# Feature projections of a two-layer decoder trunk: three 256-column matmuls into one accumulator, and tiles moved by 192 bytes

## The chip, the cores and the metric

The kernel runs on one core of a Trainium2 chip. The metric is the device time of one execution in microseconds (us). PE is the tensor engine's matmul stream, PEld its weight loads, DVE the vector engine, ACT the scalar engine, POOL GpSimd, SP the engine that issues most DMAs.

## The reference

Two layers, 256 tokens, 1024 features, all in float32. Cut to what matters:

```python
for l in range(2):
    proj = x @ w_in[l]                      # 1024 -> 6912 features: q, k, v of two attentions, three conv inputs, three gates
    y_a = sliding_window_attention(a_q, a_k, a_v, sinks, slopes)
    u = b_c * b_h                           # gated short convolution, 512 channels, 3 taps
    y_b = b_b * (u[-2] * cw[0] + u[-1] * cw[1] + u * cw[2])
    y_c = moba_attention(c_q, c_k, c_v, slopes)      # 256 tokens: one causal block
    mix = (sigmoid(g_a) * (y_a @ w_br_a) + sigmoid(g_b) * (y_b @ w_br_b) + sigmoid(g_c) * (y_c @ w_br_c)) @ w_out[l]
    x = layer_norm(sqrt(2) * x + mix)
    ffn = (silu(x @ w_gate) * (x @ w_up)) @ w_down   # 1024 -> 2816 -> 1024
    x = layer_norm(sqrt(2) * x + ffn)
```

## The kernel before

**Numbers in two parts.** Every operand of a projection is held as two tiles of the type float32r: a high part, written by ACT (`halve`, `parts`), and a low part, the difference, made by DVE. A product is the sum of three matmuls: high by high, low by high, high by low.

**Pieces.** The weights lie in memory as 140 pieces (70 a layer) of 128 x 2048 float32, 1 MB each, in the order of their use. SP loads a piece into one of three `raw` tiles; ACT and DVE split it in two chunks of 1024 columns into one of four pairs `wh`, `wl` (line 182 and 183). Four pieces a layer that are needed later are split into other tiles, `wA` and `wB`. A task list, `Plan`, simulates the engines as the program is written and so sets the order of the instructions of ACT and DVE between the matmuls; `pe_time` is its cost of a matmul.

**Which operand moves.** A matmul holds 128 x 128 values in the array (the stationary operand, fetched by a weight load) and streams another (the moving operand) past it. Five kinds of stage differ in that:

- `whole` (accumulator `acc`, 72 pieces): one piece is 2 x 8 blocks of 128 x 128 weights, each of them stationary; the features of all 256 tokens move. `xx` holds high and low part of a block beside each other, so one matmul of 512 columns multiplies both by the high weights, into the two halves of a bank of 512 columns, and one of 256 columns adds the high features by the low weights to the second half. `gather` then lets ACT copy the second half into `low` (line 278) and DVE add it to the first (line 355). These pieces are the queries and keys, the convolution's inputs, two of the three gates and 18 of the 22 column blocks of the FFN.
- `branch` (`br`) and `merge` (`gc`): the same blocks by `trio`, three matmuls of 256 columns into one half bank; `y` or `xx` moves.
- `half_pair` (`hp`): the features of 128 tokens are stationary, 256 weight columns move; three matmuls a block.
- `project` (`pr`) and the values (`cv`): features stationary (`mx`, `hidA`, `hidB`, `xx`), 512 (in one place 256) weight columns move.
- the attention's small matmuls (`s`, `tp`, `yp`), placed between pieces of `whole`.

**The short convolution.** `conv_h` gathers one factor, `conv_c` gathers the other and POOL multiplies them (line 702); POOL's `taps` follow (lines 710 to 713); `conv_b` gathers the gate, POOL multiplies (line 721) and ACT and DVE split the product.

**Where the tiles start.** Tiles lie one behind another in each partition. The start of those that matmuls read, in bytes modulo 256, as the built program has them (blocks within a tile are multiples of 256 bytes apart):

| tile | before | after the change |
|---|---|---|
| `wh`, `wl` (weights) | 160 | 0 |
| features in `xx` | 160 | 192 |
| `y` | 192 | 192 |
| `hidA` | 192 | 0 |
| `hidB`, `mx` | 160 | 0 |
| `wA`, `wB` | 192 | 0 |

From these the text uses the **lead**: the start of the moving operand less the start of the stationary operand of the next matmul (the one that is loaded while it streams), modulo 256. Lead in bytes, before and after: `acc` 0 and 192; `br` 32 and 192; `gc` 0 and 192; `hp` 0 (32 where `wB` moves) and 64; `cv` 0 and 64; `pr` 0 for `wh` over `mx` and `hidB`, 224 over `hidA`, 32 for `wA` and `wB`, and 0 for all of them after.

Of the kernel before, what the change touches and what calls it, by code (L numbers as in the profile page):

```python
# [9 lines left out]
FT = mybir.dt.float32  # L10
FR = mybir.dt.float32r
AF = mybir.ActivationFunctionType
# [4 lines left out]
P = 128  # L17
D = 1024
S = 256
L = 2  # L20
KD = D // P
# [10 lines left out]
ALPHA = (2 * L) ** 0.25  # L32
LN_EPS = 1e-5
FAR = 1.0e30


def slope(i):
# [10 lines left out]


class Plan:  # L50
    """Orders the instructions of each engine by an estimate (us) of when they can start."""

    HOP = 0.09

# [44 lines left out]


def pe_time(cols):
    return cols / 2400 + 0.0025


def dve(n):
    return "V", 0.07 + n * 0.00104


def act(n):
    return "A", 0.07 + n * 0.00083  # L110
# [3 lines left out]
def trunk(ctx: ExitStack, tc: tile.TileContext, x, xt, w, sinks, conv, ln, out):  # L114
    nc = tc.nc
# [7 lines left out]
    ctx.enter_context(tc.manual_schedule(engines={ENG.PE, ENG.DVE, ENG.Activation, ENG.SP}))  # L123
    T = Plan()

    # Weight pieces: loaded and split ahead of their use, in the order in which they are used.
    place = {}
    for l in range(L):
        place[l * PER_LAYER + N_IN + N_BR + N_OUT - 1] = "A"
# [78 lines left out]
        del ready[j]  # L208
        open_splits()

    # Tensor-engine work that waits for a result, issued once the engine has got that far.
    waiting, rounds = [], []
    busy = [0]

# [27 lines left out]
    banks = {"mm": [], "o": []}  # L242

    def bank(shape, tag, name):
        """The next PSUM bank; its last reader four tiles ago is waited for."""
        t = ps.tile(shape, FT, tag=tag, name=name)
        if len(banks[tag]) >= 4:
            for task in banks[tag].pop(0):
                T.finish(task)
        banks[tag].append([])  # L250
        return t, banks[tag][-1]

    def mm(acc, a, b, start, stop):
        nc.tensor.matmul(acc, a, b, start=start, stop=stop)  # L254
        T.pe += pe_time(int(np.prod(b.shape[1:])))
# [17 lines left out]
    def halve(dst, src, n):  # L273
        return [act(n) + (lambda: nc.scalar.activation(dst[0], src, AF.Copy),),  # L274
                dve(n) + (lambda: nc.vector.tensor_sub(dst[1], src, dst[0].bitcast(FT)),)]  # L275

    def copy(dst, src, n):
        return [act(n) + (lambda: nc.scalar.activation(dst, src, AF.Copy),)]  # L278

    def mul(dst, a, b, n):  # L280
        return [dve(n) + (lambda: nc.vector.tensor_mul(dst, a, b),)]
# [1 line left out]
    rings = {}  # L283

    def scratch(tag, bufs=2, shape=(P, S)):
        """A work tile for the next task; the task that had its slot before is that task's to wait for."""
        ring = rings.setdefault(tag, [])
        had = ring.pop(0) if len(ring) >= bufs else None
        ring.append(None)
        claims.append((ring, len(ring) - 1, had))  # L290
        return work.tile(list(shape), FT, tag=tag, name=tag, bufs=bufs)
# [3 lines left out]
    def after(users, ops, needs=(), **k):  # L295
        t = T.add(ops, needs=list(needs) + [had for _, _, had in claims if had], **k)
        for ring, i, _ in claims:
            ring[i] = t
        claims.clear()
        users.append(t)  # L300
        return t

    xx = keep.tile([P, KD, 2, S], FR, name="xx")
    xk = [xx[:, k] for k in range(KD)]
    xs = keep.tile([P, KD, S], FT, tag="z", name="xs")
    steps = [slice(0, 1), slice(1, 2), slice(2, 4), slice(4, 6), slice(6, 8)]
    load(steps)
# [4 lines left out]
    for k in steps:  # L312
        n = (k.stop - k.start) * S
        for op in halve((xx[:, k, 0, :], xx[:, k, 1, :]), xs[:, k, :], n) + halve(
# [13 lines left out]

    far_c = const.tile([P, 3, P], FT)
    far_w = const.tile([P, 3, P], FT)  # L330
    nc.gpsimd.iota(far_c[:, 0, :], pattern=[[-1, P]], base=0, channel_multiplier=1,
                   allow_small_or_imprecise_dtypes=True)
    nc.gpsimd.iota(far_c[:, 1:3, :], pattern=[[-1, 2 * P]], base=P, channel_multiplier=1,
# [15 lines left out]
        mm(acc, src[k][:, 0, t], wl, False, False)  # L349
        mm(acc, src[k][:, 1, t], wh, False, last)  # L350

    def gather(dst, acc):
        low = scratch("low", 3)
        return copy(low, acc[:, 1, :], S) + [
            dve(S) + (lambda: nc.vector.tensor_add(dst, acc[:, 0, :], low),)]  # L355

    def whole(done, by_step=False):
        j = take()
        wh, wl = duo(j)
        accs = [bank([P, 2, S], "mm", "acc") for m in range(2)]  # L360
        order = [(m, k) for m in range(2) for k in range(KD)]
        if by_step:
            order.sort(key=lambda mk: mk[1])
        for m, k in order:
            acc, users = accs[m]
            mm(acc, wh[:, m, k, :], xk[k], k == 0, False)
            mm(acc[:, 1, :], wl[:, m, k, :], xk[k][:, 0, :], False, k == KD - 1)
            if k == KD - 1:
                if m:
                    drop(j)  # L370
                done(m, acc, users)
                tick()
# [12 lines left out]
        return acc, users  # L385

    class Round:
        """A pair of heads: keys and queries split, head a's high part on its own 64 partitions."""

        def __init__(self, when, q, k, new_k, xq, xk, scores):  # L390
            self.when, self.q, self.k, self.new_k, self.xq, self.xk = when, q, k, new_k, xq, xk
# [202 lines left out]
            tick()  # L594

    def mixer_tiles():
        mix = keep.tile([P, 18 * S + 4 * (S + 2)], FT, tag="mix", name="mix")
        aq, ak, av, cq, ck, cv = [
            mix[:, lo * S:hi * S].rearrange("p (k s) -> p k s", k=k)
            for lo, hi, k in ((0, 4, 4), (4, 5, 1), (5, 6, 2), (6, 10, 4), (10, 14, 4), (14, 18, 2))]  # L600
        return aq, ak[:, 0, :], av, cq, ck, cv, mix[:, 18 * S:].rearrange("p (k s) -> p k s", k=4)

    def qkv_pair(tiles, n):
        aq, ak, av, cq, ck, cv, up = tiles
# [22 lines left out]
    mix = None  # L627
    for l in range(L):
        aq, ak, av, cq, ck, cv, up = tiles = mix or mixer_tiles()
        y = keep.tile([P, 3, 4, 2, S], FR, tag="A", name="y")  # L630
        nc.gpsimd.memset(up[:, :, 0:2], 0.0)
        at["kv"] = []
        at["n"] = 4 if l else 6

        def heads(dst, j, mark, by_step=False):
            def done(m, acc, users):
                at[mark].append(after(users, gather(dst[:, 2 * j + m, :], acc)))

            whole(done, by_step)

# [48 lines left out]
        for j in range(2):  # L689
            hh = {}  # L690

            made, zs = {}, {}

            def conv_h(m, acc, users):
                hh[m] = scratch("hh")
                made[m] = after(users, gather(hh[m], acc))

            def conv_c(m, acc, users):
                i = 2 * j + m
                t = scratch("t1")  # L700
                u = up[:, i, 2:]
                made[2 + m] = after(users, gather(t, acc) + [("G", 0.69, lambda: nc.gpsimd.tensor_mul(u, t, hh[m]))],
                                    needs=[made[m]])
                z = zs[m] = scratch("t2")

                tap = [cw[:, l, 4 * n + i:4 * n + i + 1].to_broadcast([P, S]) for n in range(3)]
                other = hh[m]

                def taps():
                    nc.gpsimd.tensor_mul(z, up[:, i, 0:S], tap[0])  # L710
                    for n in (1, 2):
                        nc.gpsimd.tensor_mul(other, up[:, i, n:S + n], tap[n])
                        nc.gpsimd.tensor_add(z, z, other)

                made[4 + m] = after([], [("G", 4.0, taps)], needs=[made[2 + m]])

            def conv_b(m, acc, users):
                i = 2 * j + m
                t = scratch("t1")
                z = zs[m]  # L720
                at["y"].append(after(users, gather(t, acc) + [("G", 0.69, lambda: nc.gpsimd.tensor_mul(z, z, t))]
                                     + halve((y[:, 1, i, 0, :], y[:, 1, i, 1, :]), z, S),
                                     needs=[made[4 + m]]))

            for part in (conv_h, conv_c, conv_b):
                whole(part)

        gs = keep.tile([P, 2, KD, S], FT, tag="B", name="gs")
        sums, raw_gates, sig = {}, {}, {}

        def gates(b):
            for n in range(4):
                def done(m, acc, users):
                    g = gs[:, b % 2, 2 * n + m, :]
                    raw_gates[b % 2, 2 * n + m] = after(users, gather(g, acc), due=6.0)

                whole(done)

        def branch(b):
# [8 lines left out]
            for n in range(2):  # L748
                j = take()
                wh, wl = [t.rearrange("p (m k c) -> p m k c", m=4, k=4) for t in ready[j]]  # L750
                for m in range(4):
# [12 lines left out]
                    else:  # L764
                        sums[i] = after(users, copy(gi, acc, S), needs=[sums[i]])
                    tick()

        def trio(acc, wh, wl, xk_, first, last):
            mm(acc, wh, xk_[:, 0, :], first, False)
            mm(acc, wh, xk_[:, 1, :], False, False)  # L770
            mm(acc, wl, xk_[:, 0, :], False, last)

        def plus(zi, t):
            return [dve(S) + (lambda: nc.vector.tensor_add(zi, zi, t),)]
# [62 lines left out]
        for f in range(4, NF):  # L837
            gu = {}

            def done(m, acc, users):  # L840
                gu[m] = scratch(("t1", "t2")[m])
                ops = gather(gu[m], acc)
                if m:
                    g, u = gu[0], gu[1]
                    sg = scratch("hh")
                    ops += [act(S) + (lambda: nc.scalar.activation(sg, g, AF.Sigmoid),)]
                    ops += mul(g, g, sg, S) + mul(g, g, u, S) + halve((hk[f][:, 0, :], hk[f][:, 1, :]), g, S)
                last_f[f].append(after(users, ops, needs=last_f[f]))

            whole(done)  # L850
# [83 lines left out]
```

## Time and profile before

| what | value |
|---|---|
| median of 3 runs | 867.36 us (867.16 to 869.5) |
| span of the profiled execution, first to last instruction | 864.6 us |
| PE busy / DVE / ACT / POOL, of the span | 99% / 73% / 56% / 8% |
| chain that ended last: PE's part | 97% |
| DMA | 155 MB, mean 179 GB/s |

The profiled execution has its span of 864.6 us; the time of a run has some more around it, 2.8 us by the median. A matmul's row has its start and a modelled end that lies behind the start of the next one, so "busy" and "mean ns of one" of matmuls overlap; what a matmul costs in a dense row is the distance from its start to the next start, here called its step.

### The profile page before, as it was taken

Reading aid. Unit: us, or ns where it says so; the run is one execution under the profiler, and the core shown is the slowest. Engines: PE = TensorE matmul, PEld = TensorE weight load, DVE = VectorE, ACT = ScalarE, POOL = GpSimd, SP = SyncE. Lnnn points to the kernel's source line nnn. Section 1 sums busy time; section 2 is a strip of 40 time slices with the busy share of each in tenths; the row PEclk is TensorE's granted clock in tenths of the full one; section 3 lists DMA queues with packets and bytes.
Section 4 is the critical chain, followed back from the end, with each engine's and each line's share of the span. In section 5 each row is a group of like instructions: output and inputs, shape, how many; then the busy total and the mean of one; then the engine's idle time right before and its main releaser. Section 6 shows DMA issues by size and latency. Waiting matters only on the chain.

```text
span 864.6 us, 13385 instructions
## 1 busy us (share of the span) xinstructions
PE 852.0 (99%) x5222; PEld 748.1 (87%) x5222; DVE 633.3 (73%) x1105; ACT 485.6 (56%) x897; POOL 71.1 (8%) x94
## 2 busy tenths in 40 slices
PE   7999999999999999999999999999999999999996
PEld 5978888999899888888898888889998988888885
DVE  5688998766876777755657899986679577777435
ACT  6657677745535666544346767776555265565320
POOL 2003620000100000000000065000000000000000
PEclk9999999999999999999999999999999999999999
DMA  8854444464754555556336343345557365555511
GB/s 295 290 187 155 141 152 146 166 223 163 276 197 159 186 191 195 191 188 227 124 105 242 140 169 124 139 154 196 195 195 249 142 238 177 175 189 196 194 49 49
DMA packets 24815, 155.02 MB, mean 179 GB/s; under 512 B 2704, under 2 KB 4528, under 8 KB 7344
## 3 DMA queue, kind: packets, MB, share of 16 engines
q1 hardware_dynamic: 23536, 149.96, 49.0%
q0 software_dynamic: 1216, 4.22, 1.5%
q8 instruction: 41, 0.67, 0.3%
q14 instruction: 22, 0.18, 0.1%
HBM read 153.11 MB, written 1.05 MB: 178 GB/s over the span
## 4 chain that ended last, share of the span: by engine, by line
PE 97%; DMA 1%; SPq 1%; DVE 1%; ACT 0%; POOLq 0%; issue 0%
PE acc L254 46%; PE pr L254 19%; PE hp L254 9%; PE br L254 8%; PE gc L254 5%; PE s L254 3%; PE cv L254 3%; PE tp L269 2%; PE yp L468 1%; DMA raw<-w 1%; PE yp L470 0%; SPq L154 0%; SPq L153 0%; DVE xtok L496 0%; DVE wl L183 0%; ACT wh L182 0%
## 5 line engine op out<-in xcount | busy, mean ns | idle before, releaser
L254 PE MATMUL acc<-xx,wh 128*128 128x512 f32 x1152 | 411.5, 400 | 5.2 <-ACT wh L274 4.9
L183 DVE TENSOR_TENSOR wl<-raw,wh 128x1024 fp32r<-128x1024 f32 x266 | 325.2, 1243 | 98.5 <-ACT wh L182 97.3
L182 ACT ACTIVATE wh<-raw 128x1024 fp32r<-128x1024 f32 x266 | 272.5, 1052 | 101.8 <-PE pr L254 48.1
L254 PE MATMUL acc<-xx,wl 128*128 128x256 f32 x1152 | 324.8, 282 | 0.2 <-DVE wl L183 0.2
L254 PEld LDWEIGHTS acc<-xx,wh 128*128 128x128 f32 x1152 | 217.6, 189 | 56.7 <-ACT wh L274 6.2
L254 PEld LDWEIGHTS acc<-xx,wl 128*128 128x128 f32 x1152 | 218.9, 190 | 1.5 <-DVE wl L275 0.9
L278 ACT ACTIVATE low<-acc 128x256 f32<-128x256 f32 x144 | 54.2, 380 | 69.7 <-PE acc L254 69.5
L254 PE MATMUL hp<-wh,xx 128*128 128x256 f32 x384 | 72.1, 285 | 0.0
L254 PE MATMUL br<-y,wh 128*128 128x256 f32 x384 | 67.9, 280 | 0.0
L254 PE MATMUL pr<-wh,hidA 128*128 128x512 f32 (+1 forms) x216 | 61.7, 370 | 0.0
L254 PEld LDWEIGHTS hp<-wh,xx 128*128 128x128 f32 x384 | 60.7, 191 | 0.1
L254 PEld LDWEIGHTS br<-y,wh 128*128 128x128 f32 x384 | 59.0, 188 | 0.1
L355 DVE TENSOR_TENSOR t<-acc,low 128x256 f32<-128x256 f32 x88 | 37.0, 420 | 29.9 <-ACT low L278 29.8
L254 PE MATMUL hp<-wl,xx 128*128 128x256 f32 x192 | 54.3, 283 | 0.0
L254 PE MATMUL br<-y,wl 128*128 128x256 f32 x192 | 53.8, 280 | 0.0
L254 PE MATMUL gc<-xx,wh 128*128 128x256 f32 x256 | 46.1, 283 | 0.0
L254 PEld LDWEIGHTS pr<-wh,hidA 128*128 128x128 f32 x216 | 39.0, 188 | 7.7
L254 PE MATMUL pr<-wh,hidB 128*128 128x512 f32 (+1 forms) x144 | 41.9, 367 | 0.0
L499 POOL TENSOR_TENSOR mv<-mv,half 128x1 f32<-128x1 f32 x8 | 7.7, 963 | 398.0 <-DVE mv L490 398.0
L254 PE MATMUL pr<-wl,hidA 128*128 128x512 f32 (+1 forms) x108 | 40.0, 370 | 0.0
L254 PEld LDWEIGHTS gc<-xx,wh 128*128 128x128 f32 x256 | 39.9, 192 | 0.0
L254 PEld LDWEIGHTS hp<-wl,xx 128*128 128x128 f32 x192 | 36.8, 192 | 0.0
(130 smaller groups left out, 1073.1 us busy)
## 6 DMA issues: line engine op xcount, KB each, us to landing
raw<-w SPq DMA_DIRECT2D x136, 1024.0 KB, 4.8
gb<-ln POOLq DMA_DIRECT2D x8, 512.0 KB, 6.1
raw<-w SPq DMA_DIRECT2D x6, 512.0 KB, 6.8
xtok<-x SPq DMA_DIRECT2D x2, 512.0 KB, 6.7
xs<-xt SPq DMA_DIRECT2D x3, 256.0 KB, 4.8
raw<-w SPq DMA_DIRECT2D x3, 256.0 KB, 5.4
out<-xtok SPq DMA_DIRECT2D x3, 256.0 KB, 2.1
xs<-xt SPq DMA_DIRECT2D x2, 128.0 KB, 2.7
```

What stands on the lines that cost most here:

```text
L182: return [act(n) + (lambda: nc.scalar.activation(wh[:, s], raw[j][:, s], AF.Copy),), dve(n) + (lambda: nc.vector.tensor_sub(wl[:, s], raw[ ...
L183: dve(n) + (lambda: nc.vector.tensor_sub(wl[:, s], raw[j][:, s], wh[:, s].bitcast(FT)),)]
L254: nc.tensor.matmul(acc, a, b, start=start, stop=stop)
L269: nc.tensor.transpose(tp[:, i, :], src(i), ident)
L278: return [act(n) + (lambda: nc.scalar.activation(dst, src, AF.Copy),)]
L355: dve(S) + (lambda: nc.vector.tensor_add(dst, acc[:, 0, :], low),)]
L468: nc.tensor.matmul(yp[los[a], :], v[:, 0, vsel[a]], pts[a][:, 0:2, :], start=True, stop=False)
L499: nc.gpsimd.tensor_tensor(mv[:, 3:4], mv[:, 2:3], half, op=OP.pow)
```

## The change

Pieces of `whole` are computed by `trio`: two matmuls of 256 columns with the high weights and one with the low weights, all three into one accumulator of 256 columns. There is no second half to add: whoever needs the result reads the accumulator. `gather` is gone: queries, keys, gates and `conv_h` copy it by ACT; `conv_c` and `conv_b` multiply it on DVE; the FFN takes the sigmoid from it on ACT and multiplies it on DVE. `xx` and `y` start 48 floats (192 bytes) into their allocation, and small tiles (`rest`, `line_up`) and a longer `mix` bring the others to starts that are multiples of 256 bytes. The planner's cost of a matmul grows by 4.2 ns.

```diff
+LINE = 64
+AHEAD = 48
 def pe_time(cols):
-    return cols / 2400 + 0.0025
+    return cols / 2400 + 0.0067
...
-    xx = keep.tile([P, KD, 2, S], FR, name="xx")
+    xx = keep.tile([P, AHEAD + KD * 2 * S], FR, name="xx")
+    xx = xx[:, AHEAD:].rearrange("p (k a s) -> p k a s", k=KD, a=2)
+    rest = keep.tile([P, LINE - AHEAD], FT, name="rest")
+    nc.gpsimd.memset(rest, 0.0)
...
+    line_up = const.tile([P, 24], FT)
+    nc.gpsimd.memset(line_up, 0.0)
...
-    def gather(dst, acc):
-        low = scratch("low", 3)
-        return copy(low, acc[:, 1, :], S) + [
-            dve(S) + (lambda: nc.vector.tensor_add(dst, acc[:, 0, :], low),)]
+    def trio(acc, wh, wl, src, first, last):
+        mm(acc, wh, src[:, 0, :], first, False)
+        mm(acc, wh, src[:, 1, :], False, False)
+        mm(acc, wl, src[:, 0, :], False, last)
...
-        accs = [bank([P, 2, S], "mm", "acc") for m in range(2)]
+        accs = [bank([P, S], "mm", "acc") for m in range(2)]
...
-            mm(acc, wh[:, m, k, :], xk[k], k == 0, False)
-            mm(acc[:, 1, :], wl[:, m, k, :], xk[k][:, 0, :], False, k == KD - 1)
+            trio(acc, wh[:, m, k, :], wl[:, m, k, :], xk[k], k == 0, k == KD - 1)
...
-        mix = keep.tile([P, 18 * S + 4 * (S + 2)], FT, tag="mix", name="mix")
+        mix = keep.tile([P, 18 * S + 4 * (S + 2) + 56], FT, tag="mix", name="mix")
...
-        y = keep.tile([P, 3, 4, 2, S], FR, tag="A", name="y")
+        y = keep.tile([P, AHEAD + 12 * 2 * S], FR, tag="A", name="y")
+        y = y[:, AHEAD:].rearrange("p (b k a s) -> p b k a s", b=3, k=4, a=2)
...
-                at[mark].append(after(users, gather(dst[:, 2 * j + m, :], acc)))
+                at[mark].append(after(users, copy(dst[:, 2 * j + m, :], acc, S)))
...
-                t = scratch("t1")
-                u = up[:, i, 2:]
-                made[2 + m] = after(users, gather(t, acc) + [("G", 0.69, lambda: nc.gpsimd.tensor_mul(u, t, hh[m]))],
-                                    needs=[made[m]])
+                made[2 + m] = after(users, mul(up[:, i, 2:], acc, hh[m], S), needs=[made[m]])
...
-                at["y"].append(after(users, gather(t, acc) + [("G", 0.69, lambda: nc.gpsimd.tensor_mul(z, z, t))]
-                                     + halve((y[:, 1, i, 0, :], y[:, 1, i, 1, :]), z, S),
+                at["y"].append(after(users, mul(z, z, acc, S) + halve((y[:, 1, i, 0, :], y[:, 1, i, 1, :]), z, S),
...
-                    raw_gates[b % 2, 2 * n + m] = after(users, gather(g, acc), due=6.0)
+                    raw_gates[b % 2, 2 * n + m] = after(users, copy(g, acc, S), due=6.0)
...
-                gu[m] = scratch(("t1", "t2")[m])
-                ops = gather(gu[m], acc)
                 if m:
-                    g, u = gu[0], gu[1]
-                    sg = scratch("hh")
-                    ops += [act(S) + (lambda: nc.scalar.activation(sg, g, AF.Sigmoid),)]
-                    ops += mul(g, g, sg, S) + mul(g, g, u, S) + halve((hk[f][:, 0, :], hk[f][:, 1, :]), g, S)
+                    g = gu[0]
+                    ops = mul(g, g, acc, S) + halve((hk[f][:, 0, :], hk[f][:, 1, :]), g, S)
+                else:
+                    g = gu[0] = scratch("g", 3)
+                    ops = [act(S) + (lambda: nc.scalar.activation(g, acc, AF.Sigmoid),)] + mul(g, g, acc, S)
```

On PE, around a step of the sliding-window attention of the first layer, before the change (`acc` is the accumulator of a piece of the convolution, `yp` and `s` are the attention's products):

```order
L254 MATMUL acc<-xx,wh 128x512
L254 MATMUL acc<-xx,wl 128x256
L468 MATMUL yp<-pt,mix 64x256 x2
L470 MATMUL yp<-pt,mix 64x128 x2
L254 MATMUL s<-xa 128x256 x2
```

The same place with the change:

```order
L256 MATMUL acc<-xx,wh 128x256 x2
L256 MATMUL acc<-xx,wl 128x256
L474 MATMUL yp<-pt,mix 64x256 x2
L476 MATMUL yp<-pt,mix 64x128 x2
L256 MATMUL s<-xa 128x256 x2
```

The 512-column matmul has become two of 256 columns; the attention's matmuls stand at the same place behind the same block of the piece.

On DVE, where the first two blocks of `conv_b` are used (first layer), before the change (`t_804` and `t_851` hold the taps of two channel blocks, `t_892` and `t_925` the gathered gates):

```order
L355 TENSOR_TENSOR t_849<-acc,low 128x256
L275 TENSOR_TENSOR xa<-mix,xa 64x256 x2
L355 TENSOR_TENSOR t_892<-acc,low 128x256
L183 TENSOR_TENSOR wl<-raw,wh 128x1024 x4
L355 TENSOR_TENSOR t_925<-acc,low 128x256
L275 TENSOR_TENSOR y<-t_804,y 128x256
```

The same place with the change (`t_887` and `t_938` hold the taps):

```order
L277 TENSOR_TENSOR xa<-mix,xa 64x256 x2
L283 TENSOR_TENSOR t_887<-t_887,acc 128x256
L185 TENSOR_TENSOR wl<-raw,wh 128x1024
L277 TENSOR_TENSOR y<-t_887,y 128x256
L185 TENSOR_TENSOR wl<-raw,wh 128x1024
L283 TENSOR_TENSOR t_938<-t_938,acc 128x256
L185 TENSOR_TENSOR wl<-raw,wh 128x1024
```

DVE's additions out of `acc` are gone; in their place stand products of POOL's taps with `acc`, and the four chunks of `wl` now stand one by one behind them.

## Rows read from the trace of the kernel before

**Rows 1.** The profile's page: busy time of each engine with its share of the span, TensorE's granted clock in 40 slices (tenths of full speed), and the engines of the chain that ended last.

```profile
PE 852.0 (99%) x5222; PEld 748.1 (87%) x5222; DVE 633.3 (73%) x1105; ACT 485.6 (56%) x897; POOL 71.1 (8%) x94
...
PEclk9999999999999999999999999999999999999999
...
PE 97%; DMA 1%; SPq 1%; DVE 1%; ACT 0%; POOLq 0%; issue 0%
```

**Rows 2.** The waits of PE, all of them: engine and line, whom it waited for, us in total, times, longest us.

```profile
PE acc L254 <- ACT wh L274: 4.9, 1, 4.9
PE acc L254 <- DVE xx L275: 0.2, 1, 0.2
PE acc L254 <- DVE wl L183: 0.2, 1, 0.2
```

**Rows 3.** The chain that ended last: its shares of the span by engine and line, and pieces of it in order of time (start us, us, what, number of matmuls).

```profile
by line: PE acc L254 46.2%; PE pr L254 19.3%; PE hp L254 9.3%; PE br L254 7.8%; PE gc L254 5.3%; PE s L254 3.1%; PE cv L254 2.5%; PE tp L269 2.3%; PE yp L468 1.1%; DMA raw<-w 0.7%; PE yp L470 0.4%; SPq L154 0.3%; SPq L153 0.3%; DVE xtok L49
...
15.35 5.69 PE acc L254 x31
21.03 8.64 PE hp L254 x72
...
85.60 0.66 PE tp L269 x6
...
105.83 8.33 PE acc L254 x48
...
164.44 33.92 PE br L254 x288
198.36 23.02 PE gc L254 x192
...
271.86 98.93 PE acc L254 x560
...
857.37 0.43 DVE xtok L481
```

**Rows 4.** PE's instructions in order of time, one after another: `gc`, then `pr` over `hidA`, `pr` over `hidB`, and `hp` with `wB` moving. Start us, us (rows with a count are merged), engine and line, operation.

```profile
203.10 0.28 PE L254 MATMUL gc<-xx,wl 128*128 128x256 f32 x1
203.22 0.40 PE L254 MATMUL gc<-xx,wh 128*128 128x256 f32 x2
203.46 0.28 PE L254 MATMUL gc<-xx,wl 128*128 128x256 f32 x1
...
379.95 0.40 PE L254 MATMUL pr<-wl,hidA 128*128 128x512 f32 x1
380.19 0.63 PE L254 MATMUL pr<-wh,hidA 128*128 128x512 f32 x2
380.65 0.40 PE L254 MATMUL pr<-wl,hidA 128*128 128x512 f32 x1
...
409.89 0.39 PE L254 MATMUL pr<-wl,hidB 128*128 128x512 f32 x1
410.12 0.62 PE L254 MATMUL pr<-wh,hidB 128*128 128x512 f32 x2
410.57 0.39 PE L254 MATMUL pr<-wl,hidB 128*128 128x512 f32 x1
...
244.23 2.03 PE L254 MATMUL hp<-wB,xx 128*128 128x256 f32 x16
```

**Rows 5.** The costliest groups by shape: operation, count, busy us and mean ns of one, idle time of its engine just before.

```profile
L254 PE MATMUL pr<-wh,hidA 128*128 128x512 f32 x168 | 53.9, 395 | 0.0
L254 PE MATMUL pr<-wh,hidB 128*128 128x512 f32 x112 | 36.3, 391 | 0.0
L254 PE MATMUL pr<-wl,hidA 128*128 128x512 f32 x84 | 33.2, 396 | 0.0
...
L254 PE MATMUL pr<-wA,mx 128*128 128x512 f32 x48 | 12.5, 396 | 0.0
L254 PE MATMUL pr<-wB,hidB 128*128 128x512 f32 x42 | 11.0, 398 | 0.0
...
L355 DVE TENSOR_TENSOR t<-acc,low 128x256 f32<-128x256 f32 x88 | 37.0, 420 | 29.9 <-ACT low L278 29.8
```

**Rows 6.** Busy time of each engine in two stretches (the second layer's attention, its FFN): stretch, its length, then PE, PEld, DVE, ACT, POOL (count), clock, DMA share, GB/s.

```profile
500.00:586.00 86.00, 86.00 (x510) 71.68 (x508) 78.25 (x177) 61.02 (x149) 26.86 (x28) 1.00 0.42 151
...
694.00:796.00 102.00, 102.00 (x579) 88.48 (x579) 75.90 (x126) 60.46 (x108) 0.00 (x0) 1.00 0.56 194
```

**Rows 7.** POOL's instructions in order of time at the first layer's convolution, from the second channel block's product to its last tap, and the wait of ACT for POOL's product with the gate (from the list of waits).

```profile
83.76 0.68 POOL L710 TENSOR_TENSOR t<-mix,cw 128x256 f32<-128x256 f32 x1
...
90.01 1.59 POOL L713 TENSOR_TENSOR t<-t,hh 128x256 f32<-128x256 f32 x1
91.68 0.81 POOL L721 TENSOR_TENSOR t<-t,t 128x256 f32<-128x256 f32 x1
...
ACT y L274 <- POOL t L721: 7.2, 4, 2.2
```

More of the change, by code (lines that the diff above doesn't have):

```diff
@@ L600, in mixer_tiles @@
             for lo, hi, k in ((0, 4, 4), (4, 5, 1), (5, 6, 2), (6, 10, 4), (10, 14, 4), (14, 18, 2))]
-        return aq, ak[:, 0, :], av, cq, ck, cv, mix[:, 18 * S:].rearrange("p (k s) -> p k s", k=4)
+        return aq, ak[:, 0, :], av, cq, ck, cv, mix[:, 18 * S:18 * S + 4 * (S + 2)].rearrange("p (k s) -> p k s", k=4)
     def qkv_pair(tiles, n):
@@ L695, in conv_h @@
                 hh[m] = scratch("hh")
-                made[m] = after(users, gather(hh[m], acc))
+                made[m] = after(users, copy(hh[m], acc, S))
             def conv_c(m, acc, users):
                 i = 2 * j + m
-                t = scratch("t1")
-                u = up[:, i, 2:]
-                made[2 + m] = after(users, gather(t, acc) + [("G", 0.69, lambda: nc.gpsimd.tensor_mul(u, t, hh[m]))],
-                                    needs=[made[m]])
+                made[2 + m] = after(users, mul(up[:, i, 2:], acc, hh[m], S), needs=[made[m]])
                 z = zs[m] = scratch("t2")
@@ L718, in conv_b @@
                 i = 2 * j + m
-                t = scratch("t1")
                 z = zs[m]
-                at["y"].append(after(users, gather(t, acc) + [("G", 0.69, lambda: nc.gpsimd.tensor_mul(z, z, t))]
-                                     + halve((y[:, 1, i, 0, :], y[:, 1, i, 1, :]), z, S),
+                at["y"].append(after(users, mul(z, z, acc, S) + halve((y[:, 1, i, 0, :], y[:, 1, i, 1, :]), z, S),
                                      needs=[made[4 + m]]))
@@ L726, in trunk @@
                 whole(part)
+        if l == 0:
+            rest = keep.tile([P, LINE - AHEAD], FT, name="rest2")
+            nc.gpsimd.memset(rest, 0.0)
         gs = keep.tile([P, 2, KD, S], FT, tag="B", name="gs")
@@ L766, in branch @@
                     tick()
[L768 to L771, printed above, removed]
         def plus(zi, t):
```

## The prediction

> **What bounds the kernel now.** I read the page first. PE is busy 99% of the span, its clock is granted at nine tenths of full speed or more in all 40 slices, and the chain that ended last is PE for 97% [rows 1]. The reader is to see that no other engine ends a stage. The waits confirm it: PE waits 5.3 us in all, 4.9 of them once, at the start, for the first split of weights [rows 2]. From 15.35 us to 857.37 us the chain is one dense row of matmuls [rows 3]; behind it lie 7.2 us of the last normalisation, before it the first loads. So the time can only change by what a matmul costs, or by a wait that PE does not have today.
>
> Work taken from DVE, ACT and POOL is therefore worth nothing by itself. Its size: of 144 gathers' additions 128 fall away on DVE and 16 become products, 0.42 us each [rows 5], 54 us, and DVE's 91% of the attention of layer two (78.25 of 86 us [rows 6]) gets lighter. I cost it at zero, since PE already hides it.
>
> Next I read the steps, from the chain's pieces. The streaming time of 256 columns at 2.4 GHz, the higher of the two clock levels, is 106.7 ns, of 512 columns 213.3; what a step has above that I call its excess.
>
> - `acc`: 46.2% of 864.6 us is 399.4 us. The chain has 31 of the first 64 matmuls [rows 3], so 33 of 2,304 lie ahead of it, and 2,271 are 1,135.5 blocks: 351.8 ns a block of 512 + 256 columns, excess 31.8. It differs by stage: 8.33 us for 48 in the attention (347.1 a block), 98.93 us for 560 in the FFN (353.3) [rows 3].
> - `br`: 33.92 us for 288, 117.8 ns a matmul, excess 11.1. `gc`: 23.02 us for 192, 119.9, excess 13.2. `hp`: 8.64 us for 72, 120.0 [rows 3].
> - `pr`: from one `wl` row to the next, three matmuls of 512 columns, 0.70 us over `hidA` and 0.68 over `hidB` [rows 4]: 233 and 227 ns, excess 20 and 13.
>
> The main reading is here: the same shape has different steps. `gc` and `br` run the same `trio` of 256-column matmuls, at lead 0 and lead 32, and differ by 2.1 ns. `hp` with `wB` moving (lead 32) takes (2.03 - 0.28)/15 = 116.7 ns [rows 4] where `hp` at lead 0 takes 120.0. `pr` over `hidA` (lead 224) and `hidB` (lead 0) differ by 7 ns with the same instruction. What differs is where moving and stationary operand start. The steps are near multiples of 6.67 ns, the time of 16 columns or 64 bytes: 120 is 18 of them, 226.7 is 34, 233.3 is 35, and the blocks of 346.7, 353.3 are 52 and 53. That looks like two streams of reads that get into each other's way in units of 64 bytes, and part of the excess would go with another lead.
>
> The Trainium skill, TensorE: Matmul & The Clock Gate, section "Step-by-step: what each phase is for", has two independent read ports for moving operand and weights, so that a lead should not matter; the pairs of rows above, 120.0 against 116.7 and 233 against 227, disagree with it here.
>
> **The change part by part.** Columns stay: 768 a block before and after.
>
> 1. *Three matmuls for two in `acc`.* This adds 1,152 matmuls, each with an excess. The unknown is the excess at lead 192; no row of 256 columns has that lead. Bounds: from above, `gc` and `hp` at lead 0, 120.0 a step. From below, the transposes `tp`, 0.66 us for six [rows 3], 110 ns each: their 128 weight columns are the fastest back-to-back loads in this trace, and a block needs three loads. Between them, lead 32 gives 117.8 and 116.7. I take 113.3, one unit of 64 bytes below the step of lead 0, 17 units instead of 18: the mean of `wB` is 17.5 units, so steps of 17 or fewer occur there already. I choose the low side of 113 to 118 because lead 192 lies 64 bytes from the collision at 0, a whole unit, and 32 lies half a unit from it. A block is then 340.0 ns: 1,135.5 x (351.8 - 340.0) = 13.4 us gained. At 120 it is 9.3 us lost, at 110 24.8 us gained.
> 2. *`br`, lead 32 to 192, and `gc`, 0 to 192*: the same trio. 576 x (117.8 - 113.3) = 2.6 us; 384 x (119.9 - 113.3) = 2.5 us. At 120: 1.3 lost and nothing; at 110: 4.5 and 3.8.
> 3. *`hp`, lead 0 to 64.* Here the weights move and the features lead by 192, the other way round. 9.3% of the span is 80.4 us, 119.7 a step for 672 (seven pairs of pieces, 96 each). I take the 116.7 of lead 32: 2.0 us. Ends: 113.3, 4.3 us gained; or worse by one unit, as the 512-column rows are off lead 0, 126.4 a step, 4.5 us lost.
> 4. *`pr`: all leads become 0.* A dense row's mean duration rises with its step [rows 5]: 395 and 396 over `hidA` and for `wA`, 398 for `wB`, against 391 over `hidB`. 252 x 4.3 + 48 x 5 + 42 x 7 = 1.6 us. `cv`, 48 matmuls of 512 columns a layer, goes from 0 to 64: nothing, at worst 96 x 6.7 = 0.6 us lost.
> 5. *Readers straight on the accumulator.* Copies that ACT made into `low` fall away, with DVE's wait for them (29.9 us ahead of line 355 [rows 5]). A bank is now held until its last reader; four banks, two a piece, leave one and a half pieces, 8 us, before PE comes back. Zero.
> 6. *A new wait:* in `conv_b` DVE multiplies POOL's taps with the accumulator, as the order shows, so DVE waits for POOL where POOL and then ACT waited before. Behind it in DVE's queue stand chunks of `wl`, and PE waits for those. POOL's taps of one channel block last from 83.76 to 91.6 us, with another block's product between them; ACT waited at most 2.2 us for them [rows 7]. POOL loses two of seven operations a block (lines 702 and 721), so the taps come earlier. With splits in a ring of four pieces, 5.4 us each, 2.2 us is hidden; if it were not, eight times 2.2 is 17.6 us.
> 7. *Planner's cost, memsets, filler tiles.* The planner's cost orders tasks of engines that PE does not wait for; the memsets are three short operations of POOL. Zero.
>
> Sum: 13.4 + 2.6 + 2.5 + 2.0 + 1.6 = 22.1 us. Span 864.6 - 22.1 = 842.5; the median of the runs lies 2.8 above the profiled span, so 845.3 us.
>
> **The rivals.**
>
> *Each matmul has its own excess, whatever the lead.* This ends on the other side. 512 + 256 columns pay 31.8 ns in two matmuls; a third pays another, and the trio costs what it costs in `gc`, 3 x 120. `acc` loses 9.3 us, `br` 1.3, the rest stays: 878 us. It decides from a step of 117.3 on, a third of 351.8. For it: `gc` and `hp` at lead 0, all at 120. Against: `br` and `wB`, below it with the same shape.
> The Trainium skill, same page, section "Back-to-back issue gap", has a like rule: columns at 2.4 GHz plus about 2.5 ns a matmul. By an estimate from it a block goes from 325.0 to 327.5 and the kernel loses 2.8 us; but the blocks of this trace take 347 and more, so its excess is not the one here.
>
> *The lead helps no more than 32 bytes do.* At 117.8 `acc` loses 1.8 us, `gc` gains 0.8, `hp` 2.0 and `pr` 1.6: 864.8, no change. At 116.7 `acc` gains 2.0, `br` 0.6, `gc` 1.2, with 3.6 of `hp` and `pr`: 860. For it: these are the only steps measured off lead 0.
>
> *Almost all excess goes.* At 110 a step: 24.8 + 4.5 + 3.8 + 3.6 = 36.7 us, 831 us. For it only the transposes.
>
> *DVE stops at POOL* (item 6): up to 17.6 us of the gain returns, 845 to 863. Against it PE's 5.3 us of waits and a lighter DVE.
>
> **How the numbers follow.** The forecast (113.3 in the trios) 0.65, with its own range 840 to 852 from item 3's ends and half a unit in `br` or `gc`; own excess 0.10; the step of lead 32 0.13, half of it within 0.3%; all excess gone 0.07; POOL 0.05. About 0.3%, 2.6 us, is what a measurement can tell from no change. Faster: 0.65 + 0.07 + 0.05 + 0.07 = 0.84; same 0.06; slower 0.10. The range leaves out the slower case and most of the 831 us case: 836 to 863.
>
> **What would show it.** In the profile after: the chain's pieces, 72 matmuls in the attention where 48 stood and 840 in the FFN where 560 stood, give the step: I expect 113.3 in both, `br` and `gc` alike, `hp` 113 to 120, `hidA` and `hidB` alike at 227. PE's waits should stay near 5 us. I am wrong if the trio's step is above 117, if `hp` rises above 120, or if PE waits for `wl` in the convolution.

## The result, and the profile after

The changed kernel takes 860.25 us (median; 859.66 to 861.85), 0.9923 of the kernel before, with a 95% interval of 0.9905 to 0.9941. It is faster by 7 us where 22 were forecast: the time lies in the range, but the size of the gain is a third of what the sum gave.

The page of the profile after: PE, DVE, ACT and POOL busy, the granted clock, the engines of the chain that ended last.

```profile
PE 844.8 (98%) x6374; PEld 797.3 (93%) x6374; DVE 583.5 (68%) x977; ACT 456.3 (53%) x809; POOL 51.4 (6%) x81
...
PEclk9999999999999999999999999999999999999998
...
PE 96%; DMA 2%; DVE 1%; ACT 0%; issue 0%; SPq 0%; POOLq 0%; POOL 0%; DVEq 0%
```

Beside [rows 1], DVE lost 50 us of work, ACT 29, POOL 20, and PE still ends the chain. So this gift to the other engines bought nothing, as forecast. The waits of the kernel after, all those of PE and the one of DVE for POOL (line waited, for whom, us in total, times, longest):

```profile
PE acc L256 <- ACT wh L276: 5.6, 3, 4.7
PE tp L271 <- DVE xtok L502: 0.7, 1, 0.7
...
DVE t L283 <- POOL t L717: 2.6, 2, 1.3
```

PE waits 6.3 us where it waited 5.3 [rows 2]. The new wait of DVE for POOL's taps is there, 2.6 us in all, and PE pays nothing for it. The 0.7 us ahead of the transposes `tp` are new: DVE waits there for `gb`, the factors of the normalisation, whose load POOL issues behind `mx` and which lands 9.55 us later (8.77 in the kernel before, where PE did not wait); the experiments meet this wait again. So the answer lies in the steps. Pieces of the chain of the kernel after (start us, us, what, number of matmuls); the startup, two attention rows, `br`, `gc`, `hp` and the FFN:

```profile
21.22 8.16 PE hp L256 x72
...
76.24 8.18 PE acc L256 x72
...
90.29 8.48 PE acc L256 x72
...
162.61 33.92 PE br L256 x288
196.53 22.61 PE gc L256 x192
...
241.96 8.48 PE hp L256 x72
...
269.16 98.94 PE acc L256 x840
```

Here is the finding: rows of the same instruction, at the same lead of 192, have two steps. 8.18 us for 72 is 113.6 ns with its slow first matmuls, 113.3 behind them; 8.48 us is 117.8. In each layer four of the six long attention rows run at 113.3 and two at 117.8. The FFN's 840 matmuls, 98.94 us, are all at 117.8, `br` (33.92) and `gc` (22.61) too. Three steps of 117.8 are 353.3 ns, what the pair of 512 and 256 columns took in the FFN before, 98.93 us [rows 3]: the costliest row of the kernel gained nothing. `br` takes 33.92 us on both sides of the change.

The 512-column rows did what was expected. Groups by shape of the kernel after (count, busy us, mean ns of one, idle):

```profile
L256 PE MATMUL pr<-wh,hidA 128*128 128x512 f32 x168 | 53.0, 390 | 0.0
L256 PE MATMUL pr<-wh,hidB 128*128 128x512 f32 x112 | 36.3, 390 | 0.0
```

`hidA` falls from 395 to the 390 of `hidB` (391 before, [rows 5]).

Summed over PE's dense rows of both traces, startup included: `acc` 412.5 to 410.0 us, `hp` 81.1 to 79.6, `br` 67.8 to 67.8, `gc` 46.0 to 45.2, `pr` of 512 columns 151.6 to 150.3, `cv` 22.3 to 22.4. These are 6.0 us of the 6.2 that the span lost (864.6 to 858.4).

### The profile page after: what moved, and what is told of

Same layout as the page of the kernel before. It is cut to its first block, busy times and chain, and to the rows that moved or that the text cites. A ratio compares the mean times of both kernels' runs of the same rounds, so it can differ in the third digit from the quotient of the medians.

```text
span 858.4 us, 15516 instructions
## 1 busy us (share of the span) xinstructions
PE 844.8 (98%) x6374; PEld 797.3 (93%) x6374; DVE 583.5 (68%) x977; ACT 456.3 (53%) x809; POOL 51.4 (6%) x81
## 4 chain that ended last, share of the span: by engine, by line
PE 96%; DMA 2%; DVE 1%; ACT 0%; issue 0%; SPq 0%; POOLq 0%; POOL 0%; DVEq 0%
PE acc L256 47%; PE pr L256 17%; PE hp L256 9%; PE br L256 8%; PE gc L256 5%; PE s L256 3%; PE cv L256 3%; PE tp L271 2%; DMA gb<-ln 1%; PE yp L474 1%; DMA xs<-xt 1%; PE yp L476 0%; DVE xtok L502 0%; DVE wA L185 0%; SPq L156 0%
## 5 line engine op out<-in xcount | busy, mean ns | idle before, releaser
L256 PE MATMUL acc<-xx,wh 128*128 128x256 f32 x2304 | 408.9, 282 | 5.6 <-ACT wh L276 5.6
L185 DVE TENSOR_TENSOR wl<-raw,wh 128x1024 fp32r<-128x1024 f32 x266 | 321.9, 1228 | 123.2 <-ACT wh L184 122.3
L256 PEld LDWEIGHTS acc<-xx,wh 128*128 128x128 f32 x2304 | 353.9, 190 | 6.7 <-ACT wh L276 6.2
L283 DVE TENSOR_TENSOR g<-g,acc 128x256 f32<-128x256 f32 x72 | 30.1, 417 | 58.7 <-PE acc L256 58.7
L429 ACT ACTIVATE prob<-prob,st 128x128 f32<-128x128 f32 x32 | 12.6, 395 | 46.3 <-DVE st L426 23.3
L256 PEld LDWEIGHTS br<-y,wl 128*128 128x128 f32 x192 | 36.0, 188 | 0.0
```

The costliest lines, as they stand in the source:

```text
L185: dve(n) + (lambda: nc.vector.tensor_sub(wl[:, s], raw[j][:, s], wh[:, s].bitcast(FT)),)]
L429: nc.scalar.activation(t[:, 0, :], t[:, 0, :], AF.Exp, bias=st[:, 2:3], scale=0.125, accum_out=st[:, 4:5])
```

## The experiments

Theory one: the step of a row of 256-column matmuls is set by the lead; at 192 there are two steps in which a row can settle, how it is entered decides, and it keeps that step. Theory two: the lead is fine, but DVE, ACT or the transfers get in PE's way in the FFN and the branches. Theory three, the rival of the prediction: the lead has no part, a matmul has its excess.

**All leads at 0.** The changed kernel without its offset.

```
-    xx = xx[:, AHEAD:].rearrange("p (k a s) -> p k a s", k=KD, a=2)
+    xx = xx[:, :KD * 2 * S].rearrange("p (k a s) -> p k a s", k=KD, a=2)
-        y = y[:, AHEAD:].rearrange("p (b k a s) -> p b k a s", b=3, k=4, a=2)
+        y = y[:, :12 * 2 * S].rearrange("p (b k a s) -> p b k a s", b=3, k=4, a=2)
```

> The changed kernel with the features in xx and y back at the start of their allocation: every lead of acc, br, gc, hp, cv and pr is 0, everything else stays. If the lead makes the step, acc, br and gc run at 120.0 ns a matmul in every row: acc 1,135.5 x (360 - 355) = about 6 us over the changed kernel's mean block, br 1.3 and gc 0.8 more, hp 1 to 3 more, so 868 to 874 us. If the gain came from the shorter work on DVE and ACT and the lead has no part, 860 us and the steps of the changed kernel.

Measured: 878.01 us, 1.0123 of before (1.0106 to 1.0139). Pieces of the chain:

```profile
78.81 8.64 PE acc L256 x72
...
167.99 34.56 PE br L256 x288
202.55 23.05 PE gc L256 x192
...
276.83 100.79 PE acc L256 x840
```

Every long row of 256-column matmuls is at 120.0 ns (8.64/72, 100.79/840). The time is above what I had written down, and is the 878 that the prediction gave for its slower rival. So at lead 0 the change costs 10.7 us: 1.3 of them lie in `br`, whose lead was 32 before (34.56 against 33.92 us a layer), nearly all the rest in `acc`. Moving `xx` and `y` by 192 bytes gives 17.8 us back, with the same instructions, and theory three falls.

**The tiles moved alone.** The kernel before with the change's offsets, and its pairs of 512 and 256 columns kept.

```
+    xx = keep.tile([P, AHEAD + KD * 2 * S], FR, name="xx")
+    xx = xx[:, AHEAD:].rearrange("p (k a s) -> p k a s", k=KD, a=2)
+        y = keep.tile([P, AHEAD + 12 * 2 * S], FR, tag="A", name="y")
+        y = y[:, AHEAD:].rearrange("p (b k a s) -> p b k a s", b=3, k=4, a=2)
```

> The kernel before with the tiles moved as in the change and nothing else: acc keeps its 512 + 256 columns and the gather, at lead 192. If the lead makes the step, br, gc, hp and pr have the steps of the changed kernel (117.8, 117.8, 113 to 118, 227), worth 0 + 0.8 + 1.5 + 1.3 us, and acc has a new pair step between 340 and 353 ns: 853 to 865 us. If only the trio matters, 867 us.

Measured: 865.09 us, 0.9979 (0.9967 to 0.999), at the upper end of what was written down.

```profile
77.48 8.48 PE acc L256 x48
...
165.47 33.92 PE br L256 x288
199.38 22.63 PE gc L256 x192
...
272.51 98.94 PE acc L256 x560
```

At lead 192 a pair takes 353.3 ns in every row (8.48/24), in the attention too, where it took 347.1 before. `br` and `gc` are at 117.8, as in the changed kernel. So of the 7 us some 2 come from the tiles alone, and 5 from the form of three matmuls at this lead, in those rows that settle at 113.3; at lead 0 the same form lost time.

**Rows by lead, PE alone.** A kernel of its own, which computes nothing of the reference: dense rows of 16 blocks over one piece of weights, each behind 6, 2 or 3 transposes, for the leads 0, 16, ... 240 (letters a to p). No other engine works beside it.

```
    for n, off in enumerate(LEADS):
        src = xx[:, off:off + 2 * PIECE].rearrange("p (k a s) -> p k a s", k=KD, a=2)
        turn(6); row("six", n, src)
        turn(2); row("two", n, src)
        turn(3); row("three", n, src)
```

> Leaves the whole model out: only PE works, on fixed tiles, in dense rows of 48 matmuls of 256 columns (trio; rows called six, two, three after as many transposes), of 512 + 256 columns (pair) and of 512 columns (wide), at 16 leads from 0 to 240 bytes (letters a to p, so m is 192). Theory one: at one lead a row can settle in more than one step, the entry decides, and it stays to the row's end: at lead 192 the rows end in 113.3 or in 117.8 each, at lead 0 in 120.0. Theory two: the step of 117.8 is made by the other engines' reads and writes during the FFN: then with PE alone all three rows of lead 192 run at 113.3.

Pieces of its chain, 48 matmuls of 256 columns a row, at leads 0, 16, 96, 112, 128, 160 and 192:

```profile
26.81 5.75 PE sixa L51 x48
...
59.45 5.70 PE sixb L51 x48
65.37 5.62 PE twob L51 x48
...
228.28 5.75 PE twog L51 x48
...
255.16 5.51 PE sixh L51 x48
...
266.71 5.51 PE threeh L51 x48
...
293.15 5.70 PE twoi L51 x48
...
352.41 5.64 PE sixk L51 x48
...
364.24 5.70 PE threek L51 x48
...
417.62 5.46 PE sixm L51 x48
423.30 5.46 PE twom L51 x48
429.09 5.46 PE threem L51 x48
```

With nobody beside it PE shows all of this: 120.0 at lead 0; at 16 and 160 rows of the same lead differ (5.70 and 5.62 us; 5.64 and 5.70); 113.3 at 192 in all three entries, and at 112, there behind some ten slower matmuls. No other lead of the sixteen comes below 116. Distance from 0 isn't the measure: 96 (120.0) and 128 (118.7) lie farther from it than 192 does. The weights start at 128 here and not at 0 (mod 256 bytes, as the program is built), so at lead 192 the moving operand starts at 64: it is the difference of the two starts that counts, not either of them. That rows of one lead differ by their entry alone speaks for theory one. That 192 gave 113.3 three times is what theory two had said, and it left open whether the kernel's slow rows are a matter of entry.

**Another entry to the FFN.** Six transposes that nobody reads, ahead of piece 4; the row of 840 begins in its second half, behind two transposes of the kernel itself.

```
+            if f == 4:
+                turn(lambda i: ident, 4)
+                turn(lambda i: ident, 2)
             whole(done)
```

> The changed kernel with six transposes of the identity, which nobody reads, ahead of the first of the 18 FFN pieces of each layer (0.66 us a layer): the interruption behind which all acc rows of the attention settle at 113.3. Theory one (the entry decides, and the step holds to the row's end): the 840 matmuls that follow run at 113.3 instead of 117.8, 3.7 us less a layer for 0.76 us of kick: 854 us. Theory two (the other engines' work in the FFN makes 117.8): the row stays or returns to 117.8 and the time is 861 to 862 us.

Measured: 854.57 us, 0.9851 (0.9835 to 0.9868).

```profile
21.88 8.49 PE hp L256 x72
...
164.00 33.92 PE br L256 x288
197.91 22.61 PE gc L256 x192
...
271.14 95.23 PE acc L256 x840
```

Six useless transposes a layer, 0.66 us together (as six in [rows 3]), make the kernel 5.7 us faster (854.57 against 860.25). All 840 matmuls are now at 113.3 (95.23/840 = 113.4), in both layers, with the same data, the same addresses and the same work on DVE, ACT and POOL. `br` and `gc`, which were not touched, stay at 117.8. Theory two falls for the FFN. One row shows more: the first of `hp` takes 8.49 us here (117.9) and took 8.16 (113.3) in the kernel after, though both programs are the same up to the first of the six transposes, much later. So the same instructions in the same order can settle in either step from one execution to another, and theory one needs a limit: the program alone does not always decide how a row is entered.

**Kinds of interruption.** One in the second block of each FFN piece: a matmul cut in two at 32 to 192 columns, or 1, 2 or 6 transposes.

```
+                    mm(acc[:, :c], wh[:, m, k, :], xk[k][:, 0, :c], False, False)
+                    mm(acc[:, c:], wh[:, m, k, :], xk[k][:, 0, c:], False, False)
```

> The changed kernel with an interruption in the second block of each FFN piece, of changing kind: the first matmul of the block cut at 128, 64, 192, 32, 96 or 160 columns into two, or one, two or six unread transposes ahead of it. Theory one: after each the row settles anew, in 113.3 or 117.8, and keeps it to the next one, the same kind from the same step giving the same outcome. Theory two: every piece ends at 117.8 whatever the kind.

One execution, 862.39 us. Pieces of the chain, two rows behind one transpose each, in the first and the second layer:

```profile
290.68 5.66 PE acc L256 x48
...
787.14 0.11 PE tp L271
787.25 5.13 PE acc L256 x45
```

The first runs at 117.8 (5.66/48 = 117.9), the second settles at 113.3 (5.13/45 = 114.0 with its first matmuls). Behind two transposes and behind six both steps occurred as well. So a kind of interruption has no outcome of its own, and the part of the expectation that said so is wrong; something else counts too. The cuts did better: those at 64, 96, 128 and 192 columns met a row at 117.8 seven times and left it at 113.3 each time, and no cut, at any of the six places, threw a row out of 113.3.

**Cuts at 160 columns**, in FFN piece 4 and in the first branch; and the same with cuts at 128 in the `hp` rows besides. Neither did what was expected.

```
+        if cut:
+            mm(acc[:, :160], wh, src[:, 0, :160], first, False)
+            mm(acc[:, 160:], wh, src[:, 0, 160:], False, False)
```

> The changed kernel with two matmuls a layer cut at 160 columns into two: in the second block of the first of the 18 FFN pieces and of the first branch. By theory one every such cut leads to 113.3, which the row keeps: 840 FFN matmuls and 480 of br and gc a layer at 113.3 instead of 117.8, 5.9 us less a layer for 0.23 us of cuts: 849 us. By theory two the rows stay at 117.8: 861 us.

> The same with one matmul in each of the 14 groups of hp matmuls cut at 128 columns as well. If hp at lead 64 settles as acc at lead 192 does, its 672 matmuls go from 117.8 in most rows to 113.3: up to 2.5 us less for 1.6 us of cuts, 848 us; if a cut there leads nowhere, 850.5 us.

Measured: 862.65 us (0.9953; 0.9933 to 0.9973) and 863.09 (0.995; 0.9937 to 0.9963). The first:

```profile
164.71 34.02 PE br L256 x289
...
271.43 98.94 PE acc L256 x840
```

The cut at 160 had only met rows at 113.3 before. From 117.8 its steps are 75, 82 and 182 ns, and the row goes on at 117.8. In the FFN it also stood ahead of the two transposes, behind which the row is entered anew. `hp` stayed at 117.8 in most rows: a cut at 128 is no sure remedy there.

**Cuts at 64 columns**, in piece 5, behind these transposes, and in the first branch.

```
-            mm(acc[:, :160], wh, src[:, 0, :160], first, False)
-            mm(acc[:, 160:], wh, src[:, 0, 160:], False, False)
+            mm(acc[:, :64], wh, src[:, 0, :64], first, False)
+            mm(acc[:, 64:], wh, src[:, 0, 64:], False, False)
...
-            whole(done, cut=f == 4)
+            whole(done, cut=f == 5)
```

> The changed kernel with one matmul of 256 columns cut into 64 and 192 at two places of each layer: in the second block of FFN piece f=5, which lies behind the two transposes that interrupt the row in piece f=4 (so 816 or so matmuls follow the cut without a break), and in the second block of the first branch, with 470 br and gc matmuls behind it. The cut at 64 was seen to turn the step from 117.8 to 113.3 ns each time that it was met at 117.8. Theory one (two steps that a row can settle in, the entry decides, the step then holds to the row's end): the FFN rows go from 98.9 to about 95.4 us, br from 33.9 to 32.7 and gc from 22.6 to 21.8, in both layers: 2 x (820 + 470) x 4.45 ns = 11.5 us less some 0.3 us for the cuts, so about 849 us. Rival one (what a row settles in hangs on the operands' own addresses and not on its entry, so br and gc can't run at 113.3 at this lead): FFN faster, br and gc as they were, about 853 us. Rival two (the cut's effect is lost again within the row, as with the cut at 160): 860 to 863 us.

Measured: 851.0 us, 0.9827 (0.9798 to 0.9857). The profiled execution is one of the two longest of six, 857.44 us:

```profile
164.38 32.79 PE br L256 x289
197.17 21.76 PE gc L256 x192
...
269.12 95.46 PE acc L256 x841
...
580.22 32.79 PE br L256 x289
613.00 21.77 PE gc L256 x192
...
688.42 99.04 PE acc L256 x841
```

`br` and `gc` run at 113.3 in both layers, beside the same work of the other engines, so these rows can, and theory two falls for them too. The FFN row of the first layer turned, that of the second didn't, behind the same cut: its steps were 29, 169, 144, 116, 118, 122, 119, 113 in the first, and 29, 175, 136, 117, 118, 118, 118 in the second. The two differ by 6 to 8 ns in the first matmuls behind the cut, and then by 4.5 ns in each of some 800; the cut at 64 is no sure remedy. Four executions lie at 849.7 to 851.5 us, two at 856.8 and 857.4. The row that stayed accounts for 3.6 us of that distance (99.04 against 95.46). PE's waits are another part, 8.7 us in this trace against 6.3 in the kernel after, 2.0 of them for the normalisation ahead of `tp`. The other executions have no trace, so what parts the two groups is not shown beyond this.

**Lead 112.** The changed kernel with its moving operands 112 bytes ahead.

```
-    xx = xx[:, AHEAD:].rearrange("p (k a s) -> p k a s", k=KD, a=2)
+    xx = xx[:, 28:28 + KD * 2 * S].rearrange("p (k a s) -> p k a s", k=KD, a=2)
```

(and `y` alike), first in one execution, then in five.

> The changed kernel with xx and y 112 bytes ahead of the weights instead of 192, everything else at its place: the only other lead at which the rows of the kernel that runs PE alone ended at 113.3. Theory one: acc, br and gc rows settle at 113.3 or in a slower step by their entry, so 850 to 866 us. Theory two: 113.3 in the attention and 117.8 in the FFN, as in the changed kernel, 860 us.

> The changed kernel with its moving operands 112 instead of 192 bytes ahead (mod 256), as looked at once before, now timed in rounds. Theory one (at lead 112 a row has only the step of 113.3 ns to settle in, at 192 two): 850.3 us again, about 0.980 to 0.982 of the kernel before, with all acc, br and gc rows at 113.3 and the hp rows, whose lead becomes 144, near 120. Rival (the one look was a lucky set of entries, and the long rows can settle at 117.8 here too): 854 us or more. Against the 64-column cuts: if both come out near 850, the lead and the entry are two ways to the same step.

Measured: 850.34 us, then 851.08 (850.0 to 854.77), 0.9815 (0.9794 to 0.9836). A trace of the five, of 853.44 us, with PE's wait for the normalisation behind it:

```profile
77.81 8.20 PE acc L256 x72
...
91.91 8.20 PE acc L256 x72
...
163.93 32.64 PE br L256 x288
196.57 21.77 PE gc L256 x192
...
241.39 8.64 PE hp L256 x72
...
268.94 95.25 PE acc L256 x840
...
640.06 11.69 DMA gb<-ln
...
PE tp L271 <- DVE xtok L502: 2.9, 1, 2.9
```

All long rows of `acc`, `br` and `gc` settle at 113.3 within ten to twelve matmuls, from whatever entry, in both traces. So the 3.1 us between the two traces (853.44 and 850.34) are not a matter of steps: PE's waits are 8.3 us in one and 6.1 in the other, mostly because `gb` took 11.69 us to land and not 9.78. In the kernel before it took 8.77 there, and PE did not wait. Of the five, the longest (854.77) lies above the 854 that the rival named; it has no trace. `hp`, whose lead is now 144, goes to 120.0 (8.64/72) and costs 1.8 us more than in the changed kernel (80.6 against 78.8 us, its pieces of both chains). This is the version to keep: by the medians it is as fast as the one with cuts at 64, beats both kernels, and adds no instruction.

## Why the prediction was right or wrong

- *What bounds the kernel* was right. PE ends the chain before and after, and the work taken from DVE, ACT and POOL is worth nothing.
- *Item 1*, the trio's step, is the step that failed: "I take 113.3", for all 1,135.5 blocks. The value occurs, and eight of the twelve long rows of the attention show it. Wrong was to take it for every row: at one lead there are two steps. In the FFN the step is 117.8: 560 blocks x 13.3 ns = 7.5 us that did not come. In the attention four of twelve long rows stayed there, 4 x 0.3 = 1.2 us. `acc` gained 2.5 us in place of 13.4; the remaining 2.2 are spread over short rows, some of them at 117.8 too, the first matmuls behind an interruption and the start of the kernel.
- *Item 2*: `br` and `gc` were to gain 5.1 us and gained 0.8, for the same reason.
- The reason given, that 192 lies a whole unit away from a collision at 0, fell with the rows by lead: 96 and 128 are farther away, and slow, and 64 is just as far on the other side, at 117.8. Of the sixteen leads only 112 and 192 came to 113.3, so that the lead chosen has this step at all was luck. Nor are the single steps multiples of 6.67 ns: 117.8 is none, only three of them, 353.3, are.
- *Item 3* (`hp`, 2.0 us): 1.5. The lead-64 step was taken as 116.7; it too is two, 8.16 and 8.48 us for 72 (113.3 and 117.8). *Item 4* (1.6 us): 1.3, and `cv` lost 0.1.
- *Items 5 to 7*, at nothing: right, as far as PE's waits show. DVE's wait for POOL came to 2.6 us and was hidden. A wait that no item had, for the load of `gb`, cost PE 0.7 us; whether the change or chance made that load slower is not shown.
- *The rivals.* "The lead helps no more than 32 bytes do" gave 864.8 us at 117.8 and 860 at 116.7. It describes the long rows, not the attention, and that the time is 860 is an accident of the mixture. That it lies within the stated range is as much luck: the range reached so far up for the rivals' sake, and the forecast's own part of it ended at 852. "Each matmul has its own excess" is what the kernel does at lead 0, 878.0 us.
- The signs were on the table: [rows 3] show the pair of the kernel before at two steps, 347.1 in the attention and 353.3 in the FFN, with the same shape and lead. I read this as a difference "by stage" and averaged it to 351.8. A row that had two steps before should have been given two after.

Still open: what in the few matmuls of an entry decides, and why a lead has the steps it has. The runs show that at lead 192 it is decided there, within some five to ten matmuls, and kept for up to 840; neither the number of transposes nor the place of a cut foretells it.

## What to carry to other kernels

When the same instruction shows two steps in one trace, forecast a row by its own step, and weigh both outcomes by the length of the rows: one row of 840 weighs nearly as much as twelve of 72. Where operands can be placed freely, measure the step over the leads with PE alone, from several entries, and choose a lead at which all entries end in the same step, not the one with the best single row. Then look at the long rows of the kernel itself: with PE alone all three entries ended at 113.3 at lead 192 too, and only the kernel showed its second step. A gain of this sort should be read from the dense rows of the chain: the mean over a span hides the rows that gained nothing.

## What the runs showed of the hardware

- The start of the moving operand against that of the next weights, mod 256 bytes, moves the step of a 256-column matmul between 113.3 and 120 ns, with the clock at its upper level throughout (granted clock 0.995 to 1.0 in these traces). With 512 columns, in the kernel with PE alone, lead 0 is the best of all (226.7 ns once settled; 229 to 237 elsewhere), while for 256 columns it is among the worst.
- A dense row can have two stable steps at one lead, 113.3 and 117.8 at 192. The difference, 13.3 ns in three matmuls (353.3 against 340.0), stays for 840 matmuls, and one matmul cut in two can turn it. At lead 112 only 113.3 was seen, in two traces of the kernel and three rows with PE alone.
- Adding six transposes a layer to a kernel that is bound by PE made it 5.7 us faster.
